# Later sums and half-width parts in a seven-product encoder: the order of three borders

## The chip, the core and the metric

The kernel runs on one core of one Trainium2 chip. The core's engines work side by side, each through its own queue in order: TensorE (PE in the profile; PEld is its loading of weights), VectorE (DVE), ScalarE (ACT), GpSimd (POOL) and SyncE (SP), which only starts DMA transfers here; POOL starts some too. An instruction waits on semaphores at the head of its queue, and everything behind it on that engine waits with it. The metric is the device time of one execution in microseconds (us).

## What is computed

Two requests of 512 and 256 tokens go through two layers with shared weights, 1024 features wide:

```python
for i in range(DEPTH):                      # DEPTH = 2
    h = rms_norm(x, norm_mix[i])
    if i % 2 == 0: x = x + window_attention(h, ...)
    else:          x = x + short_conv(h, conv_w_in, conv_w, conv_w_out)
    h = rms_norm(x, norm_mlp[i])
    x = x + jnp.square(jax.nn.relu(h @ mlp_w_up[i])) @ mlp_w_down[i]      # 1024 -> 4096 -> 1024
    gate = jax.nn.sigmoid(rms_norm(x, norm_ple[i]) @ ple_w_gate[i])
    x = x + (p[i] @ ple_w_proj[i]) * gate
return rms_norm(x, final_norm)
```

`short_conv` splits `h @ w_in` into three parts b, c and u, filters `z = c * u` over three neighbouring tokens and returns `(b * conv) @ w_out`. All of it is in float32.

## The kernel before

**Layout.** Everything is held transposed: 8 blocks of 128 features on the partitions, T = 768 tokens in the free dimension, in two halves of H = 384 columns. Each float32 operand is split in a high part (ACT copies it with rounding) and a low part (DVE subtracts the high part); a product is three matmuls, high by high, high by low and low by high.

**Seven products.** The large products are made of 2 x 2 blocks of weights and tokens, with seven block products in place of eight. For weights (class `Weights7`) the sums are made on DVE from two raw tiles: `sums32` (two adds of 128x512, L479 and L480) and `sums14` (L484 and L485). `high(group)` is an ACT copy (L504), `low(group)` a DVE subtraction (L532), `added(group)` makes the low part by a DMA that adds, on POOL's queue. The tokens' sums (class `Sums`, for the MLP's activations `Acts`) are `t13` (L408, L409) and `t42` (L413, L414), two DVE instructions each, and their `high(i)` (L418) and `low(i)` (L424) are 768 columns wide; `high(0)` and `low(0)` serve the products s1 and s3, `high(1)` and `low(1)` s2 and w22. `highx` and `lowx` (L454, L463) do the same for the plain operand of w12 and s4.

**The order on the engines.** Inside `tc.manual_schedule` ACT, PE and DVE do their instructions in the order in which the program writes them; SP and POOL are not in that list. One MLP step `up(u, ...)` (L1355) does the products w11, s3, s2, w12, s1, w22, s4 of 12 matmuls each. w11 and s2 and then s1 and s4 go to the PSUM bank `a`; copies of it on ACT start `c` (for w12) and `d` (for w22); s3 goes to `b` and is copied to `p`. The output halves are `y2[:, H:] = a + p` behind s1 (L1389), `y1[:, :H]` from `c`, `y2[:, :H] = d + p` behind w22 (L1405), and `y1[:, H:]` from `a` behind s4; `rectified` (L1146) is the squared ReLU's first half with the norm's factor, `squared` (L1149) the second. s4 adds to the bank `a` that L1389 reads. Between these, a list `pend` holds the eight or nine steps that turn the last step's outputs into operands; `late(n)` does n of them, the last two being `low(0)` and `low(1)`. `v` stands for the next step's weights.

`up` steps come in pairs: an even one, then two `down` steps with the outputs of the pair before it, then an odd one. Each layer has 14 `up` steps of this form (u = 2 to 15), 7 of them even. In `down` (L1418) each product is made for two output blocks; the two `b` tiles of s3 take the two PSUM banks of the tag "B", which an `up` step uses for `b` and `d`. The last `up` (u = 15, `final`) hands its `Acts` to `down_first` (L1510) through the list `aside`; `down_first` makes its operands while it already multiplies, and adds to the residual x in L1457.

**The border of the first gated layer and the convolution** is in `ple` (L1724). A gate is a product of 48 matmuls; `steps(i, gp)` returns `times` (DVE reads the PSUM banks, two instructions, L1746), `sigmoid` (ACT, L1749), `added` (two products with the projection, L1689, and the sum into x, L1752) and `block`, which makes the next norm's operand of that feature block (`plain_block`: L367, L368 or, for m >= 4, L372 and L373) and adds its square to the norm's sum (`square`, L257, L258). `steps` also starts the load of the projection on SP, into one of two tiles. `nxt.copied(2, 6)` scales two blocks (L389) for a `Sums`. The last three gates (i = 5, 6, 7, which are the blocks 6, 3 and 7) are ordered by hand, from L1766. The convolution follows at once: `plain` (L2068) multiplies all eight blocks, in the order 0, 4, 1, 5, 2, 6, 3, 7, by `c`'s "direct" weights (48 matmuls) and then by its "second" weights (48), adds up the squares on PE (`ss`, from the high and low parts `ah` and `al`, L105 and L106), and the first step `seven` (L2103) begins, whose s4 waits for the reading of `a` in `low` (L2051).

Of the kernel before, what the change touches and what calls it, by code (L numbers as in the profile page):

```python
# [11 lines left out]
F32 = mybir.dt.float32  # L12
# [8 lines left out]
KB = D // P  # L21
# [27 lines left out]
def trunk_kernel(ctx: ExitStack, tc: tile.TileContext, a: dict, out: bass.AP):  # L49
# [392 lines left out]
    class Acts(Sums):  # L442
# [14 lines left out]
        def lowx(self, i):  # L457
            if i == 0:
                hi, lo = self.x1
                dve.tensor_tensor(lo, self.q1[:, :H], hi.bitcast(F32), ALU.subtract)  # L460
            else:
                hi, lo = self.x2
                dve.tensor_tensor(lo[:], self.q2[:], hi[:].bitcast(F32), ALU.subtract)  # L463

    class Weights7:

# [669 lines left out]
    def mlp(l, norm, nxt, w, places, early, product=None, begun=None, more_gates=()):  # L1136
# [31 lines left out]
        def late(n=1):  # L1168

            for _ in range(n):  # L1170
                if pend:
                    pend.pop(0)()
# [182 lines left out]
        def up(u, w, make):  # L1355


            first, final = u == PLAIN[l], u == 2 * NG - 1
            w.low("s32")
            w.split("s14")  # L1360
            v = make()
            seven = isinstance(v, Weights7)
            a = bank("A", "a")[:, :H]
            product7(a, w, "w11", xs, True)
            c = bank("A" if first else "C", "c")[:, :H]
            act.activation(c, a, AF.Copy)
            late(len(pend) - 5)
            w.split("w22")
            late()
            b = bank("A" if first else "B", "b")[:, :H]  # L1370
            product7(b, w, "s3", xs, True)
            p = big("p")[:, :H]
            act.activation(p, b, AF.Copy)
            if seven:
                v.sums32()
            product7(a, w, "s2", xs, False)
            d = bank("B", "d")[:, :H]
            act.activation(d, a, AF.Copy)
            late(2)
            if seven:  # L1380
                v.sums14()
                (v.sum_added if final else lambda: v.high("s32"))()
            late()
            product7(c, w, "w12", xs, False)
            if seven:
                v.high("direct")
            product7(a, w, "s1", xs, False)
            y1, y2 = big("y1"), big("y2")
            dve.tensor_tensor(y2[:, H:], a, p, ALU.add)  # L1389
            rectified(y1, c, 0, H, ALU.max)  # L1390
            if final:
                e = chunk_acts(u, y1, y2)
                act.activation(y1[:, :H], y1[:, :H], AF.Square)
                e.highx(0)
            if seven:
                v.low("direct")
            late()
            if seven:
                v.low("s32")
            if final:  # L1400
                e.lowx(0)
            product7(d, w, "w22", xs, False)
            if seven:
                v.added("w22")
            dve.tensor_tensor(y2[:, :H], d, p, ALU.add)  # L1405
            rectified(y2, y2[:], 0, T, ALU.min)
            if final:
                squared(y2)
                e.highx(1)
            product7(a, w, "s4", xs, False)  # L1410
            rectified(y1, a, H, T, ALU.max)
            if final:
                aside.append(e)
            else:
                pend.extend([lambda: squared(y2)] + acts_of(u, y1, y2, y1))
            return v
# [93 lines left out]
        def down_first(w, make, top, low, products, copies, added, third, less):  # L1510


            e = aside.pop()
            a = [bank("A", "a")[:, :H] for _ in range(2)]
            products(a, "w11", True)
            e.lowx(1)
            c = copies("C", a)
            act.activation(e.q1[:, H:], e.q1[:, H:], AF.Square)
            e.t13()
            e.high(0)  # L1520
            e.t42()
            products(c, "w12", False, True)
            e.low(0)
            e.high(1)
            e.low(1)
            w.split("s14")
            v = make()
            p = third()
            added(top, 0, c, ALU.add)
            products(a, "s2", False)  # L1530
            d = copies("B", a)
            v.sums32()
            v.high("direct")
            v.sums14()
            v.high("s32")
            products(a, "s1", False)
            added(low, H, a, ALU.subtract)
            v.low("direct")
            products(d, "w22", False)
            v.added("w22")  # L1540
            added(low, 0, d, ALU.subtract)
            products(a, "s4", False)
# [181 lines left out]
    def ple(norm, nxt, w2, gps, parts, ss):  # L1724
# [39 lines left out]
        gp = product(PAIRED[5], weights(5))  # L1764
        with tc.manual_schedule(engines={ET.Activation, ET.PE, ET.DVE}):
            w6 = weights(6)  # L1766
            times, sigmoid, added, block = steps(5, gp)
            times()
            raw = fetch(a["gate"][0, PAIRED[7]])
            whi, wlo = (wp.tile([P, CH], F32R, tag=f"w{p}", name=f"w{p}", bufs=2) for p in ("hi", "lo"))  # L1770
            act.activation(whi[:], raw[:], AF.Copy)
            sigmoid()
            added()
            dve.tensor_tensor(wlo[:], raw[:], whi[:].bitcast(F32), ALU.subtract)
            w7 = blocks(whi[:], KB), blocks(wlo[:], KB)
            block()
            gp = product(PAIRED[6], w6)
            c = conv_weights(0, 0, True)
            sums = nxt.copied(2, 6)
            sums.t13()  # L1780
            sums.t42()
            times, sigmoid, added, block = steps(6, gp)
            gp = product(PAIRED[7], w7)
            c.high("direct")
            times()
            c.low("direct")
            sigmoid()
            c.high("second")
            added()
            c.low("second")  # L1790
            sums.high(0)
            block()
            sums.high(1)
            v = conv_weights(1, 0)
            times, sigmoid, added, block = steps(7, gp)
            m = KB - 1
            times()
            sums.low(0)
            nxt.copied(m - KB // 2)
            sigmoid()  # L1800
            sums.low(1)
            added()
            nxt.plain_block(m, x(m))
            v.sums32()
            sums = nxt.copied(m)
            v.high("direct")
            sq = big("sq")
            act.activation(sq[:], x(m), AF.Square)
            v.low("direct")
            dve.tensor_tensor(nxt.acc, nxt.acc, sq[:], ALU.add)  # L1810
            nxt.last = nxt.gated
            nxt.table()
            sums.t13()
            sums.high(0)
            v.high("s32")
            sums.t42()
            parts = nxt.acc_parts()
            sums.high(1)
            sums.low(0)
            sums.low(1)  # L1820
            v.low("s32")
            v.sums14()
        return c, v, parts

# [486 lines left out]
```

## Time and profile before

| | us |
|---|---|
| median of 3 runs | 1590.61 (1590.45 to 1590.70) |
| the profiled execution | 1591.22 |
| its span, first to last instruction | 1589.4 |
| VectorE busy in it | 1357.7 |
| ScalarE busy in it | 982.2 |

The mean granted clock of TensorE in the profiled execution was 0.994. "Granted clock" is the share of its full rate that the throttle let TensorE run at; a window's row gives it beside the busy times of the engines. A timeline's row gives the start from the beginning of the span, the duration, the engine, the line, the operation, output and inputs, their shape, how many instructions were merged, and in brackets the idle time ahead of it with what ended it. Matmuls are pipelined: they start every 0.16 us and last 0.33 each, and their ends are modelled.

### The profile page before, as it was taken

The numbers are of one execution on the slowest core, as the hardware profiler recorded it, in microseconds if no ns is written. First come the engines' busy times: TensorE is split into PE (matmuls) and PEld (weight loads), VectorE is DVE, ScalarE is ACT, GpSimd is POOL, SyncE is SP. The second block draws the span as 40 slices with busy tenths as digits, with TensorE's granted clock in tenths as the row PEclk, the third lists the DMA queues.
The fourth block names the chain that finished last, engine by engine and source line by source line (L and its number), as shares of the span: only waits on it lengthen the run. The fifth ranks groups of instructions, "written<-read, shape, count | busy, mean of one in ns | idle before, by whom it ended". The sixth has DMA issues, their size and how long they took to land.

```text
span 1589.4 us, 24597 instructions
## 1 busy us (share of the span) xinstructions
PE 1543.9 (97%) x9375; PEld 1489.7 (94%) x9375; DVE 1357.7 (85%) x2244; ACT 982.2 (62%) x1566; POOL 151.0 (9%) x172
## 2 busy tenths in 40 slices
PE   9999999999999999999989999999999999999996
PEld 7988889999999999999989999999999999999885
DVE  7599898898889889889898887869888988988986
ACT  7478766876566656667755344556656665665754
POOL 0211000011111111110000000000111111111000
PEclk9999999999999999999999999999999999999998
DMA  8854412445654644556522212122564554456522
GB/s 278 216 135 134 132 52 91 128 100 129 137 120 120 140 115 105 129 137 152 147 60 80 80 67 85 63 78 69 138 137 114 128 139 102 108 137 140 138 78 103
DMA packets 72694, 188.39 MB, mean 119 GB/s; under 512 B 8144, under 2 KB 26064, under 8 KB 72576
## 3 DMA queue, kind: packets, MB, share of 16 engines
q1 hardware_dynamic: 45440, 139.89, 28.3%
q0 software_dynamic: 27136, 46.93, 16.7%
q8 instruction: 73, 1.20, 0.3%
q14 instruction: 45, 0.37, 0.1%
HBM read 143.02 MB, written 10.48 MB: 97 GB/s over the span
## 4 chain that ended last, share of the span: by engine, by line
PE 61%; DVE 22%; ACT 10%; issue 4%; DMA 4%; SPq 0%; DVEq 0%; ACTq 0%
PE a L180 28%; PE mm L180 7%; PE b L180 6%; PE B L180 4%; PE C L180 4%; PE c L180 3%; PE d L180 2%; DVE t L424 2%; PE pt L847 1%; ACT y L1149 1%; PE gate L180 1%; PE p L180 1%; DVE act L463 1%; DVE pr L1689 1%; PE O L857 1%
## 5 line engine op out<-in xcount | busy, mean ns | idle before, releaser
L180 PE MATMUL a<-xs,whi 128*128 128x384 f32 x624 | 116.0, 329 | 11.2 <-DVE y L1389 9.9
L180 PEld LDWEIGHTS a<-xs,whi 128*128 128x128 f32 x624 | 102.5, 189 | 16.4 <-DVE y L1389 13.8
L180 PE MATMUL a<-t,zhi 128*128 128x384 f32 x568 | 109.5, 326 | 0.0
L180 PE MATMUL a<-t,whi 128*128 128x384 f32 x568 | 109.3, 326 | 0.0
L180 PE MATMUL b<-t,zhi 128*128 128x384 f32 x552 | 106.7, 326 | 0.3 <-DVE t L424 0.3
L180 PE MATMUL a<-act,whi 128*128 128x384 f32 x512 | 104.3, 326 | 0.0
L1475 POOL DMA_DIRECT2D x<-p x56 | 68.0, 1215 | 367.2 <-DVE x L1457 216.0
L504 ACT ACTIVATE whi<-sum 128x1024 fp32r<-128x1024 f32 x71 | 74.9, 1055 | 41.9 <-PE a L180 39.1
L532 DVE TENSOR_TENSOR wlo<-wraw,whi 128x1024 fp32r<-128x1024 f32 x74 | 90.1, 1218 | 10.9 <-ACT whi L504 10.9
L180 PEld LDWEIGHTS a<-t,whi 128*128 128x128 f32 x568 | 94.9, 189 | 0.6 <-ACT d L1565 0.6
L180 PEld LDWEIGHTS a<-t,zhi 128*128 128x128 f32 x568 | 95.1, 189 | 0.4 <-DVE t L424 0.4
L180 PEld LDWEIGHTS b<-t,zhi 128*128 128x128 f32 x552 | 92.3, 189 | 0.9 <-DVE t L424 0.9
L504 ACT ACTIVATE vhi<-wraw 128x512 fp32r<-128x512 f32 x71 | 44.4, 625 | 75.3 <-PE B L180 64.3
L504 ACT ACTIVATE zhi<-sum 128x1024 fp32r<-128x1024 f32 x71 | 74.8, 1054 | 22.2 <-DVE sum L480 22.2
L532 DVE TENSOR_TENSOR wlo<-sum,whi 128x1024 fp32r<-128x1024 f32 x71 | 86.5, 1218 | 2.2 <-ACT whi L504 2.2
L1457 DVE TENSOR_TENSOR x<-x,a 128x384 f32<-128x384 f32 x128 | 67.3, 549 | 23.6 <-PE a L180 11.8
L180 PEld LDWEIGHTS a<-act,whi 128*128 128x128 f32 x512 | 86.6, 189 | 0.3
L532 DVE TENSOR_TENSOR zlo<-sum,zhi 128x1024 fp32r<-128x1024 f32 x69 | 84.0, 1217 | 0.0
L504 ACT ACTIVATE whi<-wraw 128x1024 fp32r<-128x1024 f32 x76 | 79.4, 1045 | 1.9
L180 PE MATMUL mm<-xs_mix,whi 128*128 128x512 f32 (+1 forms) x320 | 77.3, 331 | 0.4 <-DVE pjs L610 0.4
L418 ACT ACTIVATE t<-y 128x768 fp32r<-128x768 f32 x64 | 52.3, 838 | 22.9 <-DVE y L409 17.3
L1457 DVE TENSOR_TENSOR x<-x,C 128x384 f32<-128x384 f32 x64 | 35.1, 553 | 35.3 <-PE C L180 29.2
(336 smaller groups left out, 4424.7 us busy)
## 6 DMA issues: line engine op xcount, KB each, us to landing
wraw<-in_up SPq DMA_DIRECT2D x64, 512.0 KB, 4.8
wraw<-in_down SPq DMA_DIRECT2D x64, 512.0 KB, 4.9
x<-p POOLq DMA_DIRECT2D x56, 384.0 KB, 6.4
wraw<-in_w_in SPq DMA_DIRECT2D x24, 512.0 KB, 3.5
vlo<-in_down POOLq DMA_DIRECT2D x32, 256.0 KB, 7.5
wraw<-in_gate SPq DMA_DIRECT2D x16, 512.0 KB, 4.1
vlo<-in_up POOLq DMA_DIRECT2D x28, 256.0 KB, 7.3
pj<-pjs SPq DMA_DIRECT2D x16, 384.0 KB, 2.8
```

Of the source, the lines that this page charges most:

```text
L180: pe.matmul(ps, lhsT=w, rhs=rhs, **flags)
L418: act.activation(t[0][:], (self.q1, self.q2)[i][:], AF.Copy)
L424: dve.tensor_tensor(lo[:], (self.q1, self.q2)[i][:], hi[:].bitcast(F32), ALU.subtract)
L463: dve.tensor_tensor(lo[:], self.q2[:], hi[:].bitcast(F32), ALU.subtract)
L504: act.activation(hi[:], src, AF.Copy)
L532: dve.tensor_tensor(lo[:], src, hi[:].bitcast(F32), ALU.subtract)
L847: pe.transpose(pt[:, h * P : (h + 1) * P], lg[h // 2][:, h % 2, b * P : (b + 1) * P], ident[:],)
L857: pe.matmul(O[:], lhsT=v, rhs=ph[:], start=b == 0, stop=False)
L1149: act.activation(t[:], t[:], AF.Square)
L1457: dve.tensor_tensor(t[:, o : o + H], t[:, o : o + H], f, op)
L1475: nc.gpsimd.dma_start(pairs[2 * h + 1][:, :, o : o + H], q, accum_op=ALU.add)
L1689: dve.tensor_tensor(q, q, natural(t[:, o:e]), ALU.mult)
```

## The change

There are four edits, all of them in the order of instructions or in their width.

In `up`, for even u, `sums14` of the next weights and one step of `pend` (it is `low(0)`) are written behind the reading of `a`; for odd u nothing moves. The last `up` rectifies `y2` in two halves, and leaves its square and its high part to `down_first`.

```diff
+            soon = u % 2
+
+            def others():
+                if seven:
+                    v.sums14()
+
+            if soon:
+                others()
             if seven:
-                v.sums14()
                 (v.sum_added if final else lambda: v.high("s32"))()
-            late()
+            if soon:
+                late()
             product7(c, w, "w12", xs, False)
             if seven:
                 v.high("direct")
             product7(a, w, "s1", xs, False)
             y1, y2 = big("y1"), big("y2")
             dve.tensor_tensor(y2[:, H:], a, p, ALU.add)
+            if not soon:
+                others()
+                late()
             rectified(y1, c, 0, H, ALU.max)
...
-            rectified(y2, y2[:], 0, T, ALU.min)
-            if final:
-                squared(y2)
-                e.highx(1)
+            for o, n in ((0, H), (H, T)) if final else ((0, T),):
+                rectified(y2, y2[:, o:n], o, n, ALU.min)
```

`down_first` makes its operands in halves of 384 columns with two new functions, in the order in which its products read them; the high part of the weights' s14 goes ahead of everything, its low part behind s3.

```diff
+        def part(self, t, i, j, low):
+
+            q, c = (self.q1, self.q2)[i], slice(H * j, H * j + H)
+            if low:
+                dve.tensor_tensor(t[1][:, c], q[:, c], t[0][:, c].bitcast(F32), ALU.subtract)
+            else:
+                act.activation(t[0][:, c], q[:, c], AF.Copy)
+
+        def tiles(self, at, names):
+
+            t = [slot(self.places[at + p], "t7") for p in range(2)]
+            self.keep(t, names)
+            return t
...
             e = aside.pop()
+            w.high("s14")
             a = [bank("A", "a")[:, :H] for _ in range(2)]
             products(a, "w11", True)
-            e.lowx(1)
-            c = copies("C", a)
-            act.activation(e.q1[:, H:], e.q1[:, H:], AF.Square)
+            c = [bank("C", "c")[:, :H] for _ in range(2)]
+            act.activation(c[0], a[0], AF.Copy)
+            act.activation(e.q2[:, :H], e.q2[:, :H], AF.Square)
+            act.activation(c[1], a[1], AF.Copy)
+            x2 = e.tiles(5, ("x21", "x22"))
+            t13 = e.tiles(0, ("t1", "t3"))
+            t42 = e.tiles(2, ("t4", "t2"))
+            e.part(x2, 1, 0, False)
+            e.part(x2, 1, 0, True)
+            for q in (e.q1, e.q2):
+                act.activation(q[:, H:], q[:, H:], AF.Square)
             e.t13()
-            e.high(0)
+            e.part(x2, 1, 1, False)
+            e.part(t13, 0, 1, False)
+            products(c, "w12", False, True)
+            e.part(x2, 1, 1, True)
+            e.part(t13, 0, 1, True)
+            e.part(t13, 0, 0, False)
             e.t42()
-            products(c, "w12", False, True)
-            e.low(0)
-            e.high(1)
-            e.low(1)
-            w.split("s14")
+            e.part(t42, 1, 1, False)
+            e.part(t42, 1, 1, True)
+            e.part(t42, 1, 0, False)
+            e.part(t13, 0, 0, True)
+            e.part(t42, 1, 0, True)
             v = make()
             p = third()
+            w.low("s14")
```

In `ple`, the reading of each gate is written right behind its product; the squares, the tokens' sums and low parts are written later. The new order, from gate 5 on (unchanged lines of the function's beginning are left out, `steps` now returns its block step unused):

```python
sigmoid()
dve.tensor_tensor(wlo[:], raw[:], whi[:].bitcast(F32), ALU.subtract)
...
added()
gp = product(PAIRED[6], w6)
times, sigmoid, added, _ = steps(6, gp)
c = conv_weights(0, 0, True)
times()
nxt.plain_block(PAIRED[5], x(PAIRED[5]))
sigmoid()
added()
nxt.square(PAIRED[5], x(PAIRED[5]))
c.high("direct")
c.low("direct")
nxt.plain_block(PAIRED[6], x(PAIRED[6]))
gp = product(PAIRED[7], w7)
sums = nxt.copied(2, 6)
times, sigmoid, added, _ = steps(7, gp)
times()
sums.t13()
sigmoid()
c.high("second")
sums.high(0)
added()
v = conv_weights(1, 0)
m = KB - 1
sums.t42()
nxt.plain_block(m, x(m))
c.low("second")
more_sums = nxt.copied(m - KB // 2, m)
sums.high(1)
sums.low(0)
sums.low(1)
nxt.square(PAIRED[6], x(PAIRED[6]))
sums = more_sums
sums.t13()
v.sums32()
v.high("direct")
sq = big("sq")
act.activation(sq[:], x(m), AF.Square)
sums.high(0)
sums.t42()
dve.tensor_tensor(nxt.acc, nxt.acc, sq[:], ALU.add)
v.low("direct")
nxt.last = nxt.gated
nxt.table()
parts = nxt.acc_parts()
v.high("s32")
sums.high(1)
sums.low(0)
v.low("s32")
sums.low(1)
v.sums14()
```

Before, gate 6 was read behind `t13` and `t42` of the sums of blocks 2 and 6, and gate 7 behind the direct and second low parts, block 3 and its square.

More of the change, by code (lines that the diff above doesn't have):

```diff
@@ L1766, in ple @@
             w6 = weights(6)
-            times, sigmoid, added, block = steps(5, gp)
+            times, sigmoid, added, _ = steps(5, gp)
             times()
@@ L1772, in ple @@
             sigmoid()
-            added()
             dve.tensor_tensor(wlo[:], raw[:], whi[:].bitcast(F32), ALU.subtract)
             w7 = blocks(whi[:], KB), blocks(wlo[:], KB)
-            block()
+            added()
             gp = product(PAIRED[6], w6)
+            times, sigmoid, added, _ = steps(6, gp)
             c = conv_weights(0, 0, True)
+            times()
+            nxt.plain_block(PAIRED[5], x(PAIRED[5]))
+            sigmoid()
+            added()
+            nxt.square(PAIRED[5], x(PAIRED[5]))
+            c.high("direct")
+            c.low("direct")
+            nxt.plain_block(PAIRED[6], x(PAIRED[6]))
+            gp = product(PAIRED[7], w7)
             sums = nxt.copied(2, 6)
+            times, sigmoid, added, _ = steps(7, gp)
+            times()
             sums.t13()
[L1781 to L1786, printed above, removed]
             sigmoid()
             c.high("second")
+            sums.high(0)
             added()
+            v = conv_weights(1, 0)
+            m = KB - 1
+            sums.t42()
+            nxt.plain_block(m, x(m))
             c.low("second")
-            sums.high(0)
-            block()
+            more_sums = nxt.copied(m - KB // 2, m)
             sums.high(1)
[L1794 to L1797, printed above, removed]
             sums.low(0)
-            nxt.copied(m - KB // 2)
-            sigmoid()
             sums.low(1)
-            added()
-            nxt.plain_block(m, x(m))
+            nxt.square(PAIRED[6], x(PAIRED[6]))
+            sums = more_sums
+            sums.t13()
             v.sums32()
-            sums = nxt.copied(m)
             v.high("direct")
@@ L1808, in ple @@
             act.activation(sq[:], x(m), AF.Square)
+            sums.high(0)
+            sums.t42()
+            dve.tensor_tensor(nxt.acc, nxt.acc, sq[:], ALU.add)
             v.low("direct")
-            dve.tensor_tensor(nxt.acc, nxt.acc, sq[:], ALU.add)
             nxt.last = nxt.gated
             nxt.table()
-            sums.t13()
-            sums.high(0)
+            parts = nxt.acc_parts()
             v.high("s32")
-            sums.t42()
-            parts = nxt.acc_parts()
             sums.high(1)
             sums.low(0)
+            v.low("s32")
             sums.low(1)
-            v.low("s32")
             v.sums14()
```

## The prediction

> **What bounds the kernel now.** I read the page's busy shares first, then the list of TensorE's own waits, then the timeline around each wait, engine by engine.
>
> ```profile
> span 1589.4 us, 24597 instructions
> ...
> PE 1543.9 (97%) x9375; PEld 1489.7 (94%) x9375; DVE 1357.7 (85%) x2244; ACT 982.2 (62%) x1566; POOL 151.0 (9%) x172
> ```
>
> TensorE (PE) is busy for 1543.9 of 1589.4 us. No matmul is added or removed, so what the change can win is PE's idle time and whatever that idle time does to its clock. The waits of PE name the places (us in total, times, longest):
>
> ```profile
> PE a L180 <- DVE y L1389: 9.9, 13, 1.6
> PE c L180 <- ACT xs L372: 4.6, 1, 4.6
> PE ss L180 <- ACT ah L105: 3.9, 1, 3.9
> PE C L180 <- ACT C L1452: 3.7, 2, 1.9
> ```
>
> The first row is the even `up` steps, the second the border of the gated layer and the convolution, the fourth `down_first`. The third (`ss`) is in the last gated layer, which the change leaves alone. At the border the windows show more than the wait:
>
> ```profile
> 818.14:822.71 4.57, 0.00 (x1) 0.01 (x1) 3.47 (x6) 1.51 (x3) 0.00 (x0) 0.90 0.03 13
> 822.71:828.68 5.97, 5.92 (x17) 5.41 (x18) 5.87 (x8) 4.20 (x5) 0.00 (x0) 0.50 0.01 3
> ```
>
> The second column is the stretch's length, the third from the end the granted clock: after 4.57 us without work PE runs 5.97 us at 0.50, which costs about 3.0 us more.
>
> **Part 1, even `up` steps.** PE's rows of one step, then VectorE's (DVE); start, duration:
>
> ```profile
> 448.09 0.81 PE L180 MATMUL a<-t,wlo 128*128 128x384 f32 x4
> ...
> 451.54 1.57 PE L180 MATMUL a<-xs,whi 128*128 128x384 f32 x8 [0.69 <-DVE y L1389]
> ...
> 456.20 0.49 PE L180 MATMUL b<-t,zlo 128*128 128x384 f32 x2
> 456.52 0.81 PE L180 MATMUL b<-t,zhi 128*128 128x384 f32 x4
> ```
> ```profile
> 448.26 0.69 DVE L480 TENSOR_TENSOR sum<-sum,wraw 128x512 f32<-128x512 f32 x1
> ...
> 450.08 0.94 DVE L424 TENSOR_TENSOR t<-y,t 128x768 fp32r<-128x768 f32 x1
> 450.94 0.54 DVE L1389 TENSOR_TENSOR y<-a,p 128x384 f32<-128x384 f32 x1
> ...
> 453.88 1.21 DVE L532 TENSOR_TENSOR zlo<-sum,zhi 128x1024 fp32r<-128x1024 f32 x1
> 455.01 0.55 DVE L1405 TENSOR_TENSOR y<-d,p 128x384 f32<-128x384 f32 x1
> ```
>
> The s1 product (`a<-t,wlo`) ends at 448.90. DVE has to read `a` (L1389) before s4 may add to it, but first does `sums14` and a low part (L424), so L1389 ends at 451.48 and s4 starts at 451.54, 0.69 us idle. Matmuls start 0.1625 us apart (42 of them, with one short wait, fill the time from 810.81 to 818.14 in part 3); s4's would have come at 450.69, so the wait and the slow first matmul behind it cost about 0.95.
>
> After the change L1389 follows L480 (ends 448.95). I allow 0.1 for the hand-over from s1, so it ends at 449.55, and s4 starts without a wait. `sums14` and L424 come behind it. **What is late next:** the rest of DVE's chain has the same work and no idle time, so it ends where it did plus about 0.1: L1405 at 455.7 instead of 455.56. But PE now arrives 0.95 sooner, and the second `b` product (456.52, new 455.57) uses the PSUM bank that L1405 reads, and `zlo` (ends 455.09, new 455.2) feeds the matmul of 456.20 (new 455.25). So about 0.25 comes back as a new wait. I take 0.7 saved per step; bounds 0.95 (nothing comes back) and 0.2 (both new waits with a restart each, DVE 0.4 later than I think). 12 steps are of this kind: 12 x 0.7 = 8.4.
>
> Two of the 14 even steps differ, the first of each layer:
>
> ```profile
> 340.43 1.57 PE L180 MATMUL a<-xs,whi 128*128 128x384 f32 x8 [1.59 <-DVE y L1389]
> ...
> 343.89 0.55 DVE L1405 TENSOR_TENSOR y<-d,p 128x384 f32<-128x384 f32 x1
> ```
> ```profile
> 1094.15 0.69 DVE L480 TENSOR_TENSOR sum<-sum,wraw 128x512 f32<-128x512 f32 x1
> ```
> ```profile
> 1094.86 0.81 PE L180 MATMUL a<-t,wlo 128*128 128x384 f32 x4
> ```
>
> In layer 0 the wait costs 1.86, but L1405 ends at 344.44, and `b` (4.98 behind s4, as above: 345.41) can't move before that: 0.9 saved, not 1.86. In layer 1 there was no wait; now L1389 stands in DVE's queue from 1094.84 until s1 ends at 1095.67, all behind it moves by 0.9, L1405 meets `b` exactly: -0.15. ScalarE (ACT) isn't touched: the moved `late()` is a DVE subtraction. **Part 1: 9.15.**
>
> **Part 2, last `up` and `down_first`**, twice. Layer 0:
>
> ```profile
> 720.88 0.97 PE L180 MATMUL C<-act,whi 128*128 128x384 f32 x4 [1.86 <-ACT C L1452]
> ...
> 731.40 0.81 PE L180 MATMUL a<-act,whi 128*128 128x384 f32 x4
> ```
> ```profile
> 720.48 0.96 DVE L463 TENSOR_TENSOR act<-y,act 128x768 fp32r<-128x768 f32 x1 [1.32 <-ACT act L454]
> 721.67 0.56 DVE L408 TENSOR_TENSOR y<-y 128x384 f32<-128x384 f32 x1 [0.23 <-ACT y L1518]
> ...
> 730.47 1.01 DVE L1457 TENSOR_TENSOR x<-x,a 128x384 f32<-128x384 f32 x2
> ```
>
> The copies into `C` stood behind a full-width square and copy on ACT; now the first goes ahead of them, and w12 starts about 1.6 sooner (the second `C` copy waits for the end of w11). PE then needs t3, t2 and the weights' s14 parts in turn; the halves come just ahead of s3, some 0.6 us late in s2. PE alone would gain 1.5. **But DVE sets the end of this step:** s4 (731.40) adds to the `a` that L1457 reads, behind `sums14`. DVE's idle 1.32 + 0.23 shrinks to about 0.85 (its first half still needs a half square and a half copy), four halvings cost it 0.24, gaps between dependent instructions close, and placing each instruction by these durations brings L1457 about 0.7 sooner; it had 0.38 to spare (the first of the pair ends about 731.0). So s4 starts 0.9 sooner: 2 x 0.9 = **1.8**, bounds 0.3 and 1.5 each. The s14 high part is moved on ACT into the time in which it waited for the square's input, and so is hidden; it is wanted only at s1.
>
> [...] The rows agree on the duration (0.55 at 384 columns, 0.96 at 768: 0.14 for a halving), but neighbours overlap by 0.08 here (L1389 starts at 450.94, L424 ends at 451.02), so a halving costs 0.06. [...]
>
> **Part 3, the border.** DVE, from reading gate 5 to the last sums, and ACT's copy for block 7:
>
> ```profile
> 800.64 0.55 DVE L1746 TENSOR_TENSOR gt<-gate,rstd_ple 128x384 f32<-128x384 f32 x1
> 802.09 1.24 DVE L1689 TENSOR_TENSOR pr<-pr,gt 128x384 f32<-128x384 f32 x2 [0.91 <-ACT gt L1749]
> 803.37 0.96 DVE L1752 TENSOR_TENSOR x<-x,pr 128x768 f32<-128x768 f32 x1
> 804.25 1.22 DVE L1774 TENSOR_TENSOR wlo<-wraw,whi 128x1024 fp32r<-128x1024 f32 x1
> 805.38 1.01 DVE L373 SCALAR_TENSOR_TENSOR xs<-x,vec,xs 128x768 fp32r<-128x768 f32 x1
> ...
> 814.85 0.61 DVE L368 SCALAR_TENSOR_TENSOR xs<-x,vec,xs 128x384 fp32r<-128x384 f32 x1
> ...
> 830.77 0.96 DVE L106 TENSOR_TENSOR al<-acc_mix,ah 128x768 fp32r<-128x768 f32 x1 [1.49 <-ACT ah L105]
> ...
> 835.13 0.68 DVE L485 TENSOR_TENSOR sum<-wraw,sum 128x512 f32<-128x512 f32 x1
> ```
> ```profile
> 821.72 0.94 ACT L372 ACTIVATE xs<-x,vec 128x768 fp32r<-128x768 f32 x1 [3.06 <-DVE x L1752]
> ```
> ```profile
> 810.81 0.33 PE L180 MATMUL c<-xs,zhi 128*128 128x384 f32 x1
> ...
> 835.35 1.46 PE L180 MATMUL a<-xs,whi 128*128 128x384 f32 x8
> ```
>
> The plain convolution has 96 matmuls from 810.81, and block 7 is wanted after 42 of them: 810.81 + 42 x 0.1625 = 817.6. It was ready at 822.7. In the new order DVE does from 801.18 on: low part of gate 7's weights 1.22, gate 5's products and sum 1.24 + 0.96, read gate 6 1.01, low part of block 6 1.01, products and sum 2.2, one square's sum 0.96 (the form of L1752), direct low part 1.22, block 3 1.14 (L368 twice), read gate 7 1.01, t13 1.1, products and sum 2.2: 15.3, less 13 overlaps of 0.08, plus about 0.4 where one needs the one before: x of block 7 at 815.9, its high part 0.97 later at 816.85, its low part at 817.9. That meets PE within 0.1 us, so the wait goes, and with it the stretch at half clock.
>
> What is late next is the norm's sum: two squares and the sum of parts now stand behind sums and low parts. DVE's work is the same, its idle 0.91 + 1.1 (the window's 4.57 less 3.47) + 1.49 goes, so its end moves from 835.81 to about 832. Placed one by one from 817.9: second low part 1.22, two low parts 1.9, a square's sum 0.96, t13 1.1, `sums32` 1.4, t42 1.1, a square's sum 0.96, direct low part 1.22, `al` 0.96, together 10.8, less the overlaps: `al` is done at 828.0; then two low parts, s32's and `sums14`, 4.0 with overlaps: 832.0. PE ends its 96 matmuls at 826.4, waits twice at `ss` (0.45 and 1.1), starts `a` at 828.5: 6.9 sooner than 835.35. DVE's backlog behind it (832.0 against 828.5; before, 835.8 against 835.35) is partly taken up by an idle 2.12 it had next, and the rest is paid at the next s4:
>
> ```profile
> 838.98 0.69 DVE L532 TENSOR_TENSOR vlo<-wraw,vhi 128x512 fp32r<-128x512 f32 x1 [2.12 <-ACT vhi L504]
> ...
> 847.25 0.55 DVE L2051 TENSOR_TENSOR low<-a,p 128x384 f32<-128x384 f32 x1
> ```
>
> DVE reaches L2051 6.1 sooner, so PE keeps **6.1**; bounds 3.5 (DVE 2.5 us slower than placed) and 8.2 (no new wait). SyncE's loads follow their buffers: gate 7's projection is asked for when gate 5's sum is done (804.3 before, 804.5 after) and read at 813.6; the second weight of the next step is released at 832.0 (`sums14`) and lands in 3.5:
>
> ```profile
> wraw<-in_w_in SPq DMA_DIRECT2D x24, 512.0 KB, 3.5
> ```
>
> at 835.5, read at about 836.4. POOL's queue has nothing moved.
>
> **Sum:** 9.15 + 1.8 + 6.1 = 17.05. The profiled execution took 1591.22 (its span and 1.8 around it), 0.6 above the median 1590.61: 1591.2 - 17.05 - 0.6 = 1573.5.
>
> **Rivals.** (a) *The even steps only move their wait.* L1405 and `zlo` are as late as the low end: 0.2 x 12 instead of 8.4 gives 1579.5. For it: DVE's chain in the step shows no idle. Against: 0.96 us lie between L1405's end and `b`. (b) *The border wait is passed on to `ss` and the first convolution steps*: 2 instead of 6.1 gives 1577.6. For it: DVE is busy 3.47 of the 4.57 us in which PE waits, so DVE is the bound there. (c) *No new waits* anywhere: 13.2 + 3 + 8.2, 1566. (d) *Slower: DVE idles ahead of the moved L1389.* DVE runs in order; if it gets there long before s1 ends, the 2.1 us of `sums14` and L424 that filled that time come too late. Each step then loses idle minus 0.85; the parts 2 and 3 are eaten up from an idle of 1.4 in all 14, and at 2.1 the time is 1590.6 - 7.9 + 14 x 1.25 = 1600. The rows say 0.05 to 0.15 in 12 steps, 0.83 in one. (e) *It does nothing*: the border's chain hangs on gate 7's own latency and the even steps on bank `b`, 1590.
>
> **How the numbers follow.** Forecast (1570 to 1577) 0.58, (a) 0.14, (b) 0.13, (c) 0.10, (d) 0.03, (e) 0.02. The range 1566 to 1581 takes in (a) and (b), and of (c) the half nearer to the forecast; it leaves out (d) and (e). A measurement of this kernel tells about 0.2% (3 us) from no change: faster 0.95 (forecast, a, b, c), same 0.02 (e), slower 0.03 (d).
>
> **What would show it.** PE's row `a <- y L1389` gone, small new ones at `b` (by L1405 or `zlo`) of 0.1 to 0.3; `C <- C` below 0.5 and s4 of `down_first` waiting for L1457; at the border no wait for L372, `ss` waiting 1 to 1.6 for `al`, a granted clock of 1.00 from 820 on, and s4 of the first convolution step waiting about 1.5 for L2051. Wrong would be: an idle DVE ahead of L1389, L372 still named by PE, or a clock of 0.50 elsewhere.

## The result, and the profile after

The changed kernel takes 1573.78 us in the median (1572.67 to 1575.06, 4 runs) against 1590.65 (1590.45 to 1590.83, 4 runs): a ratio of 0.9894, with a 95% interval from 0.9877 to 0.9911. It is faster by 16.9 us, where 17.05 were forecast. The sum came out better than its terms: the three edits won 15 us by the traces; of the rest, the experiments show one part to be chance and leave the other open.

The page of the profiled execution after (1572.73 us):

```profile
span 1571.0 us, 24631 instructions
PE 1541.3 (98%) x9375; PEld 1485.6 (95%) x9375; DVE 1356.4 (86%) x2252; ACT 983.3 (63%) x1574; POOL 150.9 (10%) x172
```

The matmuls are the same 9375. Their number is the handle for the rest of this document: the k-th matmul of one trace is the k-th of the other, and the difference of their starts, read along the program, says where time was won or lost. TensorE's waits after (us in total, times, longest):

```profile
PE ss L180 <- ACT ah L105: 2.3, 2, 2.1
PE b L180 <- DVE v L317: 1.8, 1, 1.8
...
PE a L180 <- DVE wlo L546: 1.0, 2, 0.8
PE ss L180 <- DVE al L106: 0.9, 2, 0.7
PE b L180 <- DVE zlo L546: 0.8, 3, 0.3
PE a L180 <- DVE x L1480: 0.7, 2, 0.4
```

The rows of before for `y`, `xs` and `C` (9.9, 4.6 and 3.7) are gone. The list leaves out waits of less than 0.1; that matters below. Lines have moved: the reading of `a` in `up` (L1389) is L1411 now, that of `d` (L1405) L1430, a low part of weights (L532) L546, the sum into x (L1457) L1480, the reading in the convolution (L2051) L2091.

**An even step.** TensorE's rows, then VectorE's, of the step shown in the prediction:

```profile
448.51 1.46 PE L180 MATMUL a<-xs,whi 128*128 128x384 f32 x8
...
451.11 0.58 PE L180 MATMUL a<-act,wlo 128*128 128x384 f32 x2
451.53 0.81 PE L180 MATMUL a<-act,whi 128*128 128x384 f32 x4
...
453.57 0.92 PE L180 MATMUL b<-t,zhi 128*128 128x384 f32 x4
```
```profile
446.81 0.56 DVE L1411 TENSOR_TENSOR y<-a,p 128x384 f32<-128x384 f32 x1
...
449.36 0.55 DVE L1160 SCALAR_TENSOR_TENSOR y<-c,rstd_mlp 128x384 f32<-128x384 f32 x1
449.83 1.21 DVE L546 TENSOR_TENSOR wlo<-wraw,whi 128x1024 fp32r<-128x1024 f32 x1
...
452.97 0.55 DVE L1430 TENSOR_TENSOR y<-d,p 128x384 f32<-128x384 f32 x1
```

L1411 is done at 447.37, 1.1 before s4, which no longer waits. From s4's first matmul to the second `b` product there are 30 matmuls, 30 x 0.1625 = 4.88 us; they took 453.57 - 448.51 = 5.06, and the matmul after that is 0.1 slow (0.92 in place of 0.81). Such a slow matmul follows nearly every wait in these traces (0.1 behind each of the 24 waits that the timeline of after shows ahead of a product of 384 columns); I count it to the wait and cut the stages behind it. So the step wins 0.96 and pays 0.29 back, in pieces too small for the list of waits (0.10 at `wlo`, 0.09 at `zlo`, 0.10 behind L1430): 0.67 net, with 0.7 forecast. Over all even steps it is 0.40 for the first and 4.03 for six more in layer 0, and -0.22 and 3.65 in layer 1: **7.86**, where 9.15 were forecast. Of the ordinary steps one, the fifth of layer 1, kept 0.32 and not 0.67: VectorE started L1411 0.39 late there, and why stays open. (The first expectations below divide the same curve a little differently, into 8.0 and 5.2.)

**down_first.** TensorE and VectorE in layer 0:

```profile
714.04 0.59 PE L180 MATMUL c<-act,whi 128*128 128x384 f32 x2 [0.24 <-ACT c L1543]
...
718.96 0.43 PE L180 MATMUL a<-t,zhi 128*128 128x384 f32 x1 [0.16 <-DVE t L469]
...
724.96 0.59 PE L180 MATMUL a<-act,whi 128*128 128x384 f32 x2 [0.36 <-DVE x L1480]
```
```profile
718.35 1.50 DVE L469 TENSOR_TENSOR t<-y,t 128x384 fp32r<-128x384 f32 x3
```

The wait of 1.86 at `C` has become one of 0.24, then one of 0.16 for a half low part, then one of 0.36 where s4 comes up against VectorE. s4 starts 0.90 and 0.88 sooner, with 0.9 forecast; the slow matmul behind its new wait takes 0.1 of each, so the two layers win **1.58**. Three halves take 1.50, so they start (1.50 - 0.56) / 2 = 0.47 apart.

**The border.** TensorE from the end of the plain convolution to s4 of the first step; windows; VectorE:

```profile
820.65 0.43 PE L180 MATMUL ss<-ah,ones 128*128 128x384 f32 x1 [0.22 <-ACT ah L105]
821.77 0.43 PE L180 MATMUL ss<-al,ones 128*128 128x384 f32 x1 [0.69 <-DVE al L106]
...
822.37 1.46 PE L180 MATMUL a<-xs,whi 128*128 128x384 f32 x8
...
826.32 1.57 PE L180 MATMUL b<-t,zhi 128*128 128x384 f32 x8 [1.84 <-DVE v L317]
...
836.17 1.46 PE L180 MATMUL a<-xs,whi 128*128 128x384 f32 x8
```
```profile
804.00:812.00 8.00, 8.00 (x50) 7.78 (x50) 7.82 (x14) 5.96 (x8) 0.00 (x0) 1.00 0.19 66
812.00:820.00 8.00, 8.00 (x51) 8.00 (x51) 7.90 (x12) 5.78 (x8) 0.00 (x0) 1.00 0.21 68
```
```profile
812.71 1.82 DVE L424 TENSOR_TENSOR t<-q,t 128x768 fp32r<-128x768 f32 x2
...
824.51 0.69 DVE L498 TENSOR_TENSOR sum<-wraw 128x512 f32<-128x512 f32 x1
825.11 0.69 DVE L499 TENSOR_TENSOR sum<-wraw,sum 128x512 f32<-128x512 f32 x1
825.71 1.02 DVE L317 TENSOR_SCALAR v<-ss 128x384 f32<-128x384 f32 x2
```

TensorE doesn't stop inside the plain convolution, and its clock is 1.00 throughout. VectorE is busy in 15.7 of those 16 us. Then come three waits, two that were forecast and a last one that was not: the first convolution step puts `b` into the PSUM bank that `ss` held, and VectorE reads `ss` (L317) only behind `sums14`. Up to s4 the border has won **5.44**, with 6.1 forecast.

**What lies outside the edits.** These three add up to 14.88, but the two traces are 18.5 apart. Of the rest, 1.12 was won ahead of the first even step that changed, and 2.49 in the last gated layer, where no line changed: there the wait for `ah` at `ss` is 3.9 before and 2.1 after.

### The profile page after: what moved, and what is told of

It is laid out like the page before. It is cut to its first block, busy times and chain, and to the rows that moved or that the text cites. A ratio compares the mean times of both kernels' runs of the same rounds, so it can differ in the third digit from the quotient of the medians.

```text
span 1571.0 us, 24631 instructions
## 1 busy us (share of the span) xinstructions
PE 1541.3 (98%) x9375; PEld 1485.6 (95%) x9375; DVE 1356.4 (86%) x2252; ACT 983.3 (63%) x1574; POOL 150.9 (10%) x172
## 3 DMA queue, kind: packets, MB, share of 16 engines
q0 software_dynamic: 27136, 46.93, 16.9%
## 4 chain that ended last, share of the span: by engine, by line
PE 71%; DVE 17%; ACT 7%; issue 3%; DMA 2%; SPq 0%; DVEq 0%; ACTq 0%
PE a L180 32%; PE mm L180 9%; PE b L180 8%; PE c L180 4%; PE d L180 4%; PE C L180 4%; PE B L180 4%; PE pt L861 1%; DVE pr L1727 1%; PE vp L180 1%; PE p L180 1%; PE O L871 1%; DVE wlo L546 1%; DVE t L424 1%; ACT L L848 1%
## 5 line engine op out<-in xcount | busy, mean ns | idle before, releaser
L180 PE MATMUL a<-t,whi 128*128 128x384 f32 x584 | 113.3, 327 | 0.0
L546 DVE TENSOR_TENSOR wlo<-wraw,whi 128x1024 fp32r<-128x1024 f32 x74 | 90.1, 1218 | 10.9 <-ACT whi L518 10.9
L546 DVE TENSOR_TENSOR wlo<-sum,whi 128x1024 fp32r<-128x1024 f32 x71 | 86.5, 1218 | 1.7 <-ACT whi L518 1.7
L1480 DVE TENSOR_TENSOR x<-x,a 128x384 f32<-128x384 f32 x128 | 67.4, 550 | 21.2 <-PE a L180 12.8
L546 DVE TENSOR_TENSOR zlo<-sum,zhi 128x1024 fp32r<-128x1024 f32 x69 | 84.1, 1218 | 0.0
L180 PE MATMUL a<-t,wlo 128*128 128x384 f32 x292 | 65.7, 326 | 0.0
L180 PE MATMUL a<-act,wlo 128*128 128x384 f32 x248 | 62.7, 332 | 1.0 <-DVE wlo L546 1.0
```

The source lines that it names most:

```text
L180: pe.matmul(ps, lhsT=w, rhs=rhs, **flags)
L546: dve.tensor_tensor(lo[:], src, hi[:].bitcast(F32), ALU.subtract)
L1480: dve.tensor_tensor(t[:, o : o + H], t[:, o : o + H], f, op)
```

## The experiments

Each was timed in five rounds beside the kernel before (medians 1590.2 to 1591.4). A difference of one or two us does not show reliably in such times, since runs of the same kernel lie up to 4 or 5 us apart; there the matmul-by-matmul comparison decides. Four kernels ran first.

### Part 1 undone

```diff
-            soon = u % 2
+            soon = True
```

> Part 1 alone undone: even up steps do sums14 and low(0) ahead of the reading of a again. My theory: by the traces of before and after, matmul by matmul, the 14 even steps gave 0.53 + 6 x 0.65 in layer 0 and 0.0 + 6 x 0.59 in layer 1, together 8.0 us, so this kernel takes 1573.8 + 8.0 = 1581.8, with TensorE's wait for the y of that line back at 9 to 10 us in 13 times, and the border and down_first as in after. Rival 1: the parts hang together (a step that ends sooner only makes the next stage wait), then it costs less than 5, below 1579. Rival 2: the 2.4 us that the end of the last gated layer won, which the change does not touch, belong to part 1 because it moves all later loads; then 8.0 + 2.4 = 10.4, 1584.2, and the wait for ah at the last ss is back near 3.9.

Measured: 1582.06 (1581.76 to 1584.47). TensorE's waits:

```profile
PE a L180 <- DVE y L1411: 10.5, 13, 2.0
PE ss L180 <- ACT ah L105: 4.5, 2, 4.3
```

The wait is back, 13 times, and the cost is 7.9 against all runs of after (median 1574.2 of 12, see below) or 8.3 against the first four (8.5 matmul by matmul). That is my theory. The second row looks like rival 2 (the end of the last gated layer moved too), but the repeats of after decide that otherwise.

### Part 2 undone

The last `up` and `down_first` as before, the rest as after (the middle of the change, backwards).

```diff
-            w.high("s14")
             a = [bank("A", "a")[:, :H] for _ in range(2)]
             products(a, "w11", True)
-            c = [bank("C", "c")[:, :H] for _ in range(2)]
...
+            e.lowx(1)
+            c = copies("C", a)
+            act.activation(e.q1[:, H:], e.q1[:, H:], AF.Square)
...
```

> Part 2 alone undone: the last up squares and copies y2 at full width and down_first has its old order. My theory: 0.9 in each layer, 1.8 us in all, so 1575.6, with a wait of 1.6 to 1.9 at C <- C twice and VectorE idle about 1.5 per layer ahead of the low part of x2. Rival 1: more than 0.9 was hidden ahead of C because PE's gain of 2.0 there was given back only by the new order's own delays (0.4 for the first C copy, 0.5 for the half t): undone costs the same 0.9 all the same, so the rival differs only in where the waits are. Rival 2: it moves the loads of the end: plus 2.4, 1578.

Measured: 1575.97 (1575.45 to 1577.06), 1.8 more than after: the theory's 1.8, in the medians. In the trace, layer 1 costs 0.8, but layer 0 costs 1.9. There the same wait of 1.86 was followed by a slow stretch. The windows of this kernel behind that wait, and of before at the same matmuls (length, then PE, PEld, DVE, ACT, POOL, granted clock):

```profile
717.10:720.50 3.40, 3.40 (x13) 3.40 (x12) 3.25 (x6) 2.43 (x3) 0.00 (x0) 0.55 0.22 40
```
```profile
722.20:725.60 3.40, 3.24 (x20) 2.94 (x20) 3.25 (x6) 2.40 (x3) 0.00 (x0) 1.00 0.23 41
```

13 matmul records against 20, at 0.55 against 1.00. I come back to this in the last section.

### The kernel after, again

> The kernel after, unchanged. Question: the last gated layer, untouched by the change, ended 2.4 us sooner after than before (the wait for ah at ss 2.06 in place of 3.88, the load of the projection landing 3.0 us behind its issue in place of 4.4), and the times of after fell in two groups, 1572.7 and 1574.9. Theory luck: the load's time varies from run to run, the times fall in the same two groups again, 2.2 apart, and a profile of 1574.9 shows the long wait of about 3.9 and a low clock behind it, one of 1572.7 the short one; kernels with a part undone show either. Theory order: the change moves the load against other transfers, then all runs of after have the short wait and kernels with a part undone the long one, whatever their part.

Measured: 1573.79 (1573.05 to 1576.57). A fourth kernel, meant to undo part 3, was by a slip the kernel after unchanged and is used as one more repeat: 1574.57 (1573.17 to 1576.30). All 12 runs of after have a median of 1574.2 and lie between 1572.67 and 1576.57, without the two groups that the first four seemed to show. Per trace, how long TensorE waited for `ah` in the last gated layer, and VectorE, just before that, for the load of a projection (`pr<-pj`):

| trace | ss waits for ah | DVE waits for pr |
|---|---|---|
| before | 3.9 | 1.2 |
| after; its repeats | 2.1; 2.0, 3.3 | 0; 0, 0.5 |
| part 1 / part 2 / part 3 undone | 4.3 / 2.0 / 3.6 | 1.4 / 0 / 0.9 |
| the five later kernels | 3.3, 3.8, 2.0, 2.1, 3.7 | 0.9, 1.0, 0, 0, 0.9 |

The same program has both the short and a long wait, and the wait is long exactly where the load was late. In the trace with part 1 undone the loads issued there took

```profile
pr<-pj SPq DMA_DIRECT2D x3, 256.0 KB, 4.5
```

4.5 us (the median of three), and in after two of them

```profile
pr<-pj SPq DMA_DIRECT2D x2, 256.0 KB, 2.9
```

2.9. So the 2.5 us at the end are one execution's luck against another's, not a gain of the change (to the trace of one repeat the difference is 0.5 there), and rival 2 of the first two experiments falls. The parts themselves repeat: by the traces of the two repeats part 1 is 8.36 and 8.33, part 2 1.58 in both, part 3 5.40 and 5.38. Only the first even step of layer 0 differs, 0.91 and 0.88 where the first trace of after shows 0.40.

### Part 3 undone

The border in its old order (the last part of the change, backwards), parts 1 and 2 kept.

```diff
             gp = product(PAIRED[6], w6)
             c = conv_weights(0, 0, True)
+            sums = nxt.copied(2, 6)
+            sums.t13()
+            sums.t42()
+            times, sigmoid, added, block = steps(6, gp)
+            gp = product(PAIRED[7], w7)
...
```

> Part 3 alone undone: the border of the first gated layer and the convolution in its old order, parts 1 and 2 kept. My theory, by the traces of before and after: 5.2 us, so 1574.1 (all runs of after) + 5.2 = 1579.3, with a wait of TensorE of 4 to 5 us for block 7 and a stretch of about 6 us at a granted clock of 0.50 behind it, no wait at bank A behind ss. Rival 1: the steps ahead of the border end some 6 us sooner with parts 1 and 2, and loads that are paced by the clock and not by the steps would then come relatively later: the wait is longer, over 6, and the cost over 7. Rival 2: the gain of the border is given back at L317 and L2091 in any case: below 3, under 1577.

Measured: 1579.03 (1578.79 to 1579.92), 4.8 more than after. TensorE's waits and the granted clock:

```profile
PE c L180 <- ACT xs L372: 4.6, 1, 4.6
```
```profile
811.80:816.45 4.65, 0.09 (x2) 0.01 (x1) 3.55 (x6) 1.59 (x3) 0.00 (x0) 0.74 0.00 0
816.45:822.30 5.85, 5.80 (x21) 5.30 (x22) 5.75 (x8) 4.08 (x5) 0.00 (x0) 0.62 0.01 3
```

The wait for block 7 is 4.6 again, although all before it ran some 6 us sooner: it belongs to the border's own order, and rival 1 falls, as does rival 2 (below 3). The slow stretch is back as well, 21 records in 5.85 us. Matmul by matmul the undoing costs 7.4 up to the end of the plain convolution and 4.7 behind s4; between lie the waits at `ss` and at bank `A`, which the old order doesn't have (3.6), less a wait at s4, which it does (0.9).

### The new wait at bank A

`sums14` of the first convolution step goes from the end of the border to behind the reading of `ss`, in the first step.

```diff
             sums.low(1)
-            v.sums14()
         return c, v, parts
...
             late(first or busy)
+            if first:
+                w.sums14()
```

> After, with sums14 of the convolution's first step moved from the end of the border to just behind the reading of ss (L317), so that the bank which b takes there comes free sooner. By the rows of after VectorE reads ss at 825.71 to 826.73 behind two adds of 0.69; without them at 824.51, so b starts 1.2 sooner and TensorE's wait for v falls from 1.8 to about 0.6. My theory: VectorE is busy without a gap from 803 to 835.8 but for 0.3, its work to the reading of a by L2091 is the same, and that has 0.4 to spare ahead of s4: so TensorE waits there instead, 0.8 to 0.9 longer, and the kernel keeps 0.3 to 0.4 of the 1.2 (1573.8, not to be told from after by its time; the trace decides at the matmul of s4). Rival: the backlog is not what sets the end; then all 1.2 are kept past s4 (1572.9).

Measured: 1573.70 (1573.01 to 1575.90). TensorE's rows:

```profile
824.67 1.57 PE L180 MATMUL b<-t,zhi 128*128 128x384 f32 x8 [0.63 <-DVE v L317]
...
835.29 1.57 PE L180 MATMUL a<-xs,whi 128*128 128x384 f32 x8 [0.61 <-DVE low L2090]
```

`b` came 1.20 sooner, and s4 lost 0.87 of it (0.77, and 0.10 for the slow matmul): 0.33 kept, as the theory said. The wait went to the next place at which TensorE meets VectorE.

### The same edit in the odd steps

In the odd steps, too, `sums14` goes behind L1411; `low(0)` stays ahead of it there (moving both was not run).

```diff
-            if soon:
+            if final:
                 others()
...
-            if not soon:
+            if not final:
                 others()
+            if not soon:
                 late()
```

> After, with sums14 moved behind the reading of a in the odd up steps too (not in the last one, and low(0) stays ahead there). VectorE arrives at that reading 0.1 us ahead of TensorE in these 13 steps; with the two adds behind it, it will sit idle 1.3 to 1.4 us ahead of it, and everything behind it comes 1.2 later. Theory A (the price of my rival d, idle less 0.85): 0.5 per step, 13 steps, 6 to 7 us slower than after, 1580.6. Theory B, from the rows of after: nothing is late in the odd step itself (the low part of s32 ends at 382.96 and is read at 385.17, that of direct at 380.95 and read at 383.22), of the 1.2 an idle of 0.61 and 0.17 in the next even step takes up 0.8, and the remaining 0.4 is paid in the even steps at wlo and b: 12 x 0.4, 5 us, 1579. Theory C: TensorE does not see it at all: 1574.

Measured: 1579.38 (1578.19 to 1580.36), 5.2 slower than after. VectorE at an odd step and in the even one behind it; TensorE in the `down` step behind that; the waits:

```profile
433.24 0.56 DVE L1411 TENSOR_TENSOR y<-a,p 128x384 f32<-128x384 f32 x1 [0.73 <-PE a L180]
...
442.25 0.56 DVE L460 TENSOR_TENSOR act<-y,act 128x384 fp32r<-128x384 f32 x1 [0.59 <-ACT act L450]
```
```profile
451.71 0.59 PE L180 MATMUL a<-act,wlo 128*128 128x384 f32 x2 [0.31 <-DVE wlo L546]
```
```profile
PE a L180 <- DVE wlo L546: 4.6, 13, 0.8
```

There are 12 odd steps of this kind, not 13 as I wrote. VectorE idles 0.73 ahead of L1411, and each even step behind pays 0.49 at `wlo`. TensorE sees nothing in the odd step itself. That is theory B in size (5) and place; theory A, the price of the prediction's rival (d), put 6 to 7 into the odd steps themselves and falls.

### The 0.3 that the even steps pay back

VectorE's chain from L1411 to L1430 has no gap, so one instruction of it that nothing wants soon is put behind L1430: the rectifying of y1's first half (L1160).

```diff
-            if not soon:
+            if soon:
+                rectified(y1, c, 0, H, ALU.max)
+            else:
                 others()
                 late()
-            rectified(y1, c, 0, H, ALU.max)
...
             dve.tensor_tensor(y2[:, :H], d, p, ALU.add)
+            if not soon:
+                rectified(y1, c, 0, H, ALU.max)
```

> After, with the rectifying of y1's first half (VectorE, 0.55, a start-to-start time of 0.47) moved in the even steps from behind low(0) to behind the sum d + p (L1430). It looks for the 0.28 us that each even step still pays in the down step behind it (0.09 at wlo of direct, 0.05 to 0.14 at zlo, 0.10 at bank b behind L1430). My theory: these three hang on VectorE's unbroken chain behind L1411, which gets 0.47 shorter up to L1430, so they go: 0.25 x 13 = 3.3 us faster than after, 1570.8, and the row of b waiting for zlo or y goes from the list. Rival: the first half of y1, or the bank that it reads, is then late itself (the squares on ScalarE start 402.34, C is wanted at 401.7): the wait moves there and nothing is won, 1574.

Measured: 1570.31 (1569.14 to 1570.67), 3.9 faster than all runs of after. The step shown above, TensorE and VectorE:

```profile
448.62 1.46 PE L180 MATMUL a<-xs,whi 128*128 128x384 f32 x8
...
453.50 0.81 PE L180 MATMUL b<-t,zhi 128*128 128x384 f32 x4
```
```profile
452.61 0.55 DVE L1431 TENSOR_TENSOR y<-d,p 128x384 f32<-128x384 f32 x1
453.08 0.54 DVE L1160 SCALAR_TENSOR_TENSOR y<-c,rstd_mlp 128x384 f32<-128x384 f32 x1
```

The 30 matmuls take 4.88 now, which is 30 x 0.1625 to the hundredth. The 0.3 are gone, in each step, and nothing else became late.

### All together, and what it ran into

The edit at bank `A` (e5 in the expectations) and the one just above (e7) together, and beside them, in `down_first`, in `seven` and at the border, what follows. This kernel is e8, the one behind it e9.

```diff
             v.high("direct")
-            v.sums14()
             v.high("s32")
             products(a, "s1", False)
             added(low, H, a, ALU.subtract)
+            v.sums14()
...
-                v.split("direct")
+                v.high("direct")
+                if not first:
+                    v.low("direct")
             product7(a, w, "s1", xs, False)
             low(kind, p, a, q, H)
+            if v:
+                v.low("direct")
...
+            dve.tensor_tensor(nxt.acc, nxt.acc, sq[:], ALU.add)
             sums.high(0)
...
             sums.t42()
-            dve.tensor_tensor(nxt.acc, nxt.acc, sq[:], ALU.add)
-            v.low("direct")
...
             parts = nxt.acc_parts()
+            v.low("direct")
```

> After, with the edits of e7 and e5 and two more. (1) So that VectorE is not late at L2091 either, the first convolution step makes the low part of the next direct weights (1.22) behind that reading and not ahead of it, and the last square's sum and its parts (al) come ahead of t42 and the low part of direct. (2) In down_first sums14 goes behind the reading of a by L1480, which s4 waits for. My theory: VectorE's order sets each of these waits; the even steps give 3.3 as in e7; at the convolution the waits at ss (0.22 and 0.69) and at bank A (0.6 left in e5) shrink to under 0.6 together and s4 does not wait for L2091, 1.6 us against after; s4 of down_first no longer waits (0.36 and a slow matmul, twice), 0.8. Together 5.7 us faster than all runs of after (1574.1): 1568.4. Rival: VectorE has no slack behind these places (busy without a gap), so what is put off is late at the next product: then little is won beyond e7, 1570.3.

Measured: 1569.08 (1568.72 to 1569.97): 1.2 below the kernel with the even steps alone, where the theory's two other terms were 1.6 and 0.8. By the traces `down_first` won more than its 0.8 (s4 no longer waits, 0.63 in each layer with the slow matmul). The convolution lost 0.46: 0.27 was won up to the first step's s4, and 0.73 lost at the second's, where the reading that s4 waits for stands behind a low part, and VectorE idles 1.66 for ScalarE ahead of that, as it did in after. VectorE, TensorE and ScalarE:

```profile
818.60 0.96 DVE L106 TENSOR_TENSOR al<-acc_mix,ah 128x768 fp32r<-128x768 f32 x1 [0.85 <-ACT ah L105]
```
```profile
824.09 1.08 PE L180 MATMUL b<-t,zhi 128*128 128x384 f32 x5 [1.77 <-DVE v L317]
...
848.70 1.57 PE L180 MATMUL a<-xs,whi 128*128 128x384 f32 x8 [0.95 <-DVE low L2093]
```
```profile
816.42 1.28 ACT L278 ACT_TABLE_LOAD   x1
817.72 0.85 ACT L105 ACTIVATE ah<-acc_mix 128x768 fp32r<-128x768 f32 x1
```

`al` was put ahead of a low part, but ScalarE's `ah` stood behind a 1.28 us table load, which in after fell into ScalarE's idle time. VectorE sat idle for 0.85, and with it the wait at bank `A` was back.

> As e8, with the border's order mended after its trace. In e8 VectorE sat idle for 0.85 ahead of al, since ScalarE's copy ah stood behind a 1.28 us preparation (L278) that used to fall into idle time, and the second step's s4 waited 0.95 for L2093 behind a low part that came 1.66 late. Now ah goes ahead of that preparation, al ahead of the low part of direct, low(1) of the last sums (0.87 start to start) goes with sums14 behind the reading of ss, and all steps of the convolution make the low part of the next direct weights behind the reading of a. My theory: al is ready at about 818.7, when TensorE comes to ss (818.5), and ss is read 1.7 sooner than in e8, so the waits at ss (0.16 and 0.56) and at bank A (1.77) shrink to under 0.5 together, and s4's three waits for L2093 (1.4 in all) to under 0.6: 2.5 to 3 us against e8 (1569.1), 1566.3. Rival: VectorE's total up to the end of the first step is the bound, so that the waits move to s4 there: 1 us or less, 1568.3.

Measured: 1568.19 (1567.69 to 1568.28), ratio 0.9856 (0.9839 to 0.9872) to before. It beats the kernels before and after. Its edit beside those of e8 (in `seven`, the low part of direct now goes behind the reading of `a` in every step):

```diff
             sums.t42()
+            parts = nxt.acc_parts()
+            nxt.table()
             v.low("direct")
-            nxt.last = nxt.gated
-            nxt.table()
-            parts = nxt.acc_parts()
...
-            sums.low(1)
-            v.sums14()
+            nxt.left = lambda: (sums.low(1), v.sums14())
```

```profile
821.85 1.57 PE L180 MATMUL b<-t,zhi 128*128 128x384 f32 x8 [0.90 <-DVE v L317]
...
832.19 1.08 PE L180 MATMUL a<-xs,whi 128*128 128x384 f32 x5 [0.32 <-DVE low L2092]
```
```profile
PE b L180 <- DVE zlo L546: 1.9, 3, 1.0
```

The first convolution step's s4 comes 1.3 sooner against e8, and at the end of the convolution this trace is 1.95 ahead, where I expected 2.5 to 3: the theory is right in the larger part. The medians are only 0.9 apart; in the two profiled executions 1.9 is lost again at the end, where the load was late in this one and not in e8's (0.9 and 0 in the table). The wait at bank `A` is halved, not gone. In the later steps s4 no longer waits for L2092, but the low part of s32 is late in its place: 1.9 where it was 0.8. To that extent the rival was right: what VectorE puts off is late at the next product.

## Why the prediction was right, and where it was not

**Part 1** (9.15 forecast; 7.86, 8.36 and 8.33 by the traces of after and its repeats; 7.9 by undoing, in the medians). The mechanism was right: the wait went, VectorE's chain behind kept its length, and part of the gain came back through `zlo` and the bank that L1405 (now L1430) reads. 0.29 came back, not 0.25, since a third instruction stood in that chain that I had not listed, the low part of direct (`wlo`, L546, 0.10 of it). For the first step of layer 0, "0.9 saved" holds in both repeats; the 0.40 of the first trace is chance, because `a<-act,wlo` waited 0.80 for L546 there and 0.5 in the repeats. The first step of layer 1 lost 0.22, with 0.15 forecast.

**Part 2** (1.8 forecast; 1.58 by trace, 1.8 by undoing). Right by its steps, but for the slow matmul behind s4's new wait, which the sum leaves out: C's wait below 0.5, and s4 waiting for VectorE's sum behind `sums14`; when `sums14` was moved behind that sum, 0.63 more was won in each layer. Two halves start 2 x 0.47 = 0.94 apart where one full-width low part (L424, two in 1.82) takes 0.87: a halving costs 0.07 here, near the 0.06 taken from the rows. By their durations two halves (0.55 each) cost 0.14 more than one full width (0.96), and neighbours overlap by some 0.08.

**Part 3** (6.1 forecast; 5.44 by trace, 4.8 by undoing). Nearly everything up to `ss` was placed right. The plain convolution starts 6.34 sooner than before,

```profile
804.47 0.33 PE L180 MATMUL c<-xs,zhi 128*128 128x384 f32 x1
```

at 804.47 in place of 810.81, and with that shift `al` was forecast for 821.7 and the end of `sums14` for 825.7; they came at 821.71 and 825.80. The step that failed is the next one: "DVE's backlog behind it ... is partly taken up by an idle 2.12 it had next, and the rest is paid at the next s4". I had it paid at the first product that reads VectorE's late *result*, and overlooked that the backlog also holds a *bank*: L317 stands behind `sums14`, and `b` of the first step takes the bank of `ss`. So 2.1 are paid at `b` (the wait of 1.84 and the matmuls next to it), nothing at s4, and the 0.9 that the wait at s4 cost before is won: net 1.2 lost behind `ss` instead of 0.8. The rest of the shortfall lies at `ss`: counted like the forecast, from the start of the plain convolution, `a` behind `ss` starts 6.64 sooner and not 6.9. VectorE comes to the reading of `a` 5.7 sooner and not 6.1; by the forecast's own rows, its end 3.8 sooner and the idle 2.12, it would have been 5.9.

**The sum.** The edits gave 14.9 (15.3 by the repeats), 2 less than forecast, and yet the median met the forecast within 0.3. That closeness is luck; the median of all 12 runs lies 0.7 above the forecast. By undoing, the parts cost 7.9 + 1.8 + 4.8 = 14.5. What makes up the other 2 us between the medians stays open: single runs of before lie between 1586.8 and 1593.5, and what the traces show outside the edits (the start, the loads at the end) varies from run to run by as much.

**The rivals.** (a), waits that only move, is far from what the even steps show (0.67, not 0.2). (b) was right in its mechanism, the border's wait is passed on to `ss` and the first step, and wrong in its size: 5 kept, not 2. (c), no new waits, and (e), no effect, fall. (d) is real where VectorE is early: in the odd steps, moving `sums14` alone costs 5.2, though the price is paid in the even steps behind them.

## What to carry to other kernels

When the wait was removed in the even steps, the waits that came next were too short for the list of waits (0.09 and 0.10 us), so compare the starts of the same matmuls in both traces, and count matmuls between two points against their pitch (30 in 5.06 where 4.88 would do). Behind a stage in which one engine is busy without a gap, list everything that the other engine takes from it, banks and buffers too, and ask of every instruction in that unbroken chain whether something wants it now; one that nothing wants soon, put behind the last one that is waited for, was worth 3.9 us here. A move of this kind costs time where the engine comes early to the instruction that is moved up (5.2 us when `sums14` was moved in the odd steps, with an idle time of 0.73 ahead of L1411), so look at the idle time ahead of it in each kind of step.

## What the runs showed of the chip beside that

After the same idle time TensorE's clock fell in one execution and not in another: behind a wait of 1.86 us it was 1.00 in before, and 0.55 for 3.4 us in the kernel with part 2 undone, at the same matmuls; in the second layer of that kernel the same wait of 1.86 left the clock alone (the matmuls behind it start 0.16 apart, where they were 0.32 apart in the slow stretch). Such a wait therefore cost 1 us more in one place than in the other (1.9 and 0.8 in the two layers of that kernel). What decides between the two was not shown. The loads of 256 KB in the last gated layer took 2.9 us in one execution and 4.5 in another, and the wait behind them differed by up to 2.3 us (2.0 to 4.3).
